# Mixer loads on GpSimd's queue with two buffers, alternating pooling inputs and gates, held-back last-block products, and a shorter VectorE chain for the samples

## The chip, the cores and the metric

One core of one Trainium2 chip runs the whole kernel. The metric is the device time of one execution in microseconds; the median of three timed runs stands for the kernel. A profile is one further execution, taken by the hardware profiler. The engines are TensorE (PE in the profile, PEld its weight loads), VectorE (DVE), ScalarE (ACT), GpSimd (POOL) and SyncE (SP, which here only issues DMAs).

## What is computed

One layer of a streaming encoder, on 1024 prompt positions and on 8 samples of 16 new positions with 1024 cached ones. All is float32.

```python
xn = rms_norm(x, norm_g)
u, g_pool, c_q, c_kv, k_r, g_mla = jnp.split(xn @ w_in, SPLIT_IDX, axis=-1)
pool_out = multiscale_pool(pool_hist, u, pos0, w_pool, pool_scale) * jax.nn.silu(g_pool)
q = (rms_norm(c_q, q_norm_g) @ w_uq).reshape(B, T, N_HEADS, D_NOPE + D_ROPE)
...
k_nope = rms_norm(kv[..., :D_NOPE], k_nope_g)
attn = chunk_causal_attention(q_nope, q_rope, k_nope, krope_all, v, q_pos, jnp.arange(S))
mla_out = attn.reshape(B, T, D_MLA) * jax.nn.silu(g_mla)
h = x + jnp.concatenate([pool_out, mla_out], axis=-1) @ w_out
gate = jax.nn.sigmoid(rms_norm(h, ple_norm_g) @ w_ple_gate + b_ple_gate)
y = h + gate * (p @ w_ple)
```

`multiscale_pool` takes 1024 channels in four groups of 256. For group g it forms the mean of the last 2, 4, 8 or 16 rows of u, subtracts u, multiplies by the group's 256 x 256 matrix and scales the channels.

## The kernel before

Positions lie along the free dimension: 1152 columns in NT = 3 blocks of TB = 384, of which the first two are prompt and the third ends with the 128 sample columns. A float32 product is made of three products of rounded halves (`split` makes the halves: ScalarE the high one, VectorE the low one; `mm3` and `product` multiply).

**Phase 1** (`phase1`) makes the input projection in tiles of 128 output channels. `kinds` lists 30 such tiles in order: 2 of ckv, 4 of cq, 8 gates gp, 8 pooling inputs u, 8 gates gm. The 2048 input rows are taken in two chunks c = 0 and 1. For the first two position blocks two tiles at a time are made with seven products in place of eight (`Quick.pair`, of 12 matmuls each, whose combined weights `sums` prepares one pair ahead). The third block, X, is multiplied plainly: 24 matmuls a tile (`product` with n = 8). In chunk 0 `keep` stores partial results; in chunk 1 `prior` loads them into PSUM and `finish` adds, applies the row factor or the SiLU, and stores the tile in DRAM. A pair with X thus has 7 x 12 + 2 x 24 = 132 matmuls, a pair without 84.

In chunk 1 the pairs 0 to 5 are made, then waiting generators are run empty and a pool of tiles is closed, then the pairs 6 to 13 and last the pair 14, whose X products come after the operands' memory is released (`left.close()`), between the second phase's first loads and its first matmuls.

**The pooling mixer** (`Pool`) runs between the products. `mixer` is called between products of the pairs 6 to 14 and does two steps per call. At pairs 8 to 11 it appends the 13 steps of one group: for each of the three blocks two `tile` (load u, sliding sums in `window`, difference d), one `mix` of the block before (L718 to L727: load the gate, six matmuls of the group's matrix, product of PSUM, scale and gate at L726, store), one `split` of d. u, the gate tile "ev", d and its halves have one buffer each; `aux_bank` has two PSUM banks. All loads and stores here are issued by SyncE, whose queue issues in order.

**Phase 2** makes keys, values and queries (`phase2`); its weights and latents come through raw tiles with two buffers. Phase 3 is the prompt's attention, phase 4 the samples' (`attend_samples`), phase 5 the output projection and the gate.

**The samples' attention** goes over 8 samples b and two halves f of four key tiles j (64 in all). Per key tile TensorE writes a three-bank PSUM tile: eight heads' keys (1024 columns), 128 score columns and 256 rotary ones. ScalarE squares the keys into sq (L1316, L1317), VectorE sums them by head (L1318), ScalarE copies the scores (L1319). Per half VectorE makes reciprocal roots (`rsqrt`, L86 to L90) and multiplies the scores of each key tile (L1324); GpSimd adds the rotary parts. `queries` splits the rotary queries of one sample into "qhl". `weigh` then does the softmax and the values of the sample before.

The order of instructions on each engine is laid down when the kernel is built, from a simulated timeline and the order in the program; on the chip each engine then runs its list in order.

Of the kernel before, what the change touches and what calls it, by code (L numbers as in the profile page):

```python
# [14 lines left out]
D = 2048  # L15
# [23 lines left out]
class K:  # L39
# [53 lines left out]
    def spread(self, pool, ps, out, r):  # L93

        nc = self.nc
        n = r.shape[1]
        rb = self.t(pool, [P, n, P], "sq")
        nc.vector.tensor_copy(rb[:], r[:].unsqueeze(2).to_broadcast([P, n, P]))
        for j in range(n):
            nc.tensor.transpose(ps[:, j * P:(j + 1) * P], rb[:, j, :], self.ident[:])  # L100
        nc.scalar.activation(out[:], ps[:, :n * P], AF.Copy)
# [151 lines left out]
def phase1(k, sc):  # L253
# [22 lines left out]
    kinds += [(n, i) for n in ("gp", "u", "gm") for i in range(8)]  # L276
# [45 lines left out]
    def factors(pool, acc, n, dim, wait=1):  # L322

        a = aux_bank()
        for j in range(n):
            nc.tensor.matmul(a[:, j:j + 1], acc[:, j * P:(j + 1) * P], k.ones[:, :1], start=True, stop=True)
        v = k.t(pool, [P, n], f"fv{n}")
        r = k.t(pool, [P, n], f"fr{n}")
        nc.vector.tensor_scalar(v[:], a[:, :n], 1.0 / dim, EPS, ALU.mult, ALU.add)
        k.rsqrt(pool, r[:], v[:], f"frs{n}")  # L330
        for _ in range(wait):
            yield
        for j in range(0, n, 3):
            k.spread(pool, aux_bank(), acc[:, j * P:(j + 3) * P], r[:, j:j + 3])
# [136 lines left out]
    def chunk(c, prior, done, between, pairs=pairs):  # L471
        def weights(m):
            return qk.sums(src[2 * m:2 * m + 2], c, c or 2 * m >= EARLY)

        W = weights(pairs[0])
        for m in pairs:
# [3 lines left out]
            qk.pair(2 * m, 2 * m + 1, A, X if c or 2 * m >= EARLY else None, W, prior, done, lambda i: between(m, i))  # L480
            W = Wn

    def prepare(m, i):
# [5 lines left out]
        if i == 1 and m == 4:  # L489
            k.later(factors(ep, R2, 3, D))  # L490
# [27 lines left out]
    def finish(i, t, ps, q):  # L518
# [18 lines left out]
        else:  # L537
            sq = k.t(lp, [P, 3, P], "sq")
            nc.scalar.activation(sq[:].rearrange("p a b -> p (a b)"), o[:], AF.Square)
            nc.vector.tensor_tensor(acc[kind, t][0][:], acc[kind, t][0][:], sq[:].rearrange("p a b -> p (a b)"), ALU.add)  # L540
# [3 lines left out]

    def ticks(m, i):
        k.tick()
# [5 lines left out]
    chunk(1, prior, finish, ticks, range(6))  # L552
    while k.queue:
        k.tick()
    ls.close()


    mp = es.enter_context(tc.tile_pool(name="p1p", bufs=1, side="right", reuse_waits="tile"))
    inv = k.t(mp, [P, 16], "inv")
    nc.sync.dma_start(inv[:], io["inv_cnt"])  # L560
    pool = Pool(k, mp, aux_bank, inv, sc, wp)

    def mixer(m, i):
        if 8 <= m < 12 and i == 0:
            g = m - 8
            for t in range(NT):
                steps.extend([lambda c=c, t=t: pool.tile(2 * g + c, t) for c in range(2)])
# [4 lines left out]
                steps.append(pool.split)  # L572
# [3 lines left out]
    chunk(1, prior, finish, mixer, range(6, KR // 2 - 1))  # L576
# [3 lines left out]
    qk.tail()  # L580
    left.close()
    yield
    for i in range(2):
        e = bank()[:, :TB]
        nc.scalar.activation(e, prior(2 * last + i, 2)[:], AF.Copy)
        qk.product(e, X, W["rest"][i], False, 8)
        finish(2 * last + i, 2, e, None)
# [61 lines left out]
class Pool:  # L649


    def __init__(self, k, pp, aux_bank, inv, sc, wp):
        self.k, self.pp, self.aux, self.inv, self.sc = k, pp, aux_bank, inv, sc
        self.wp, self.hl, self.d = wp, [None, None], [None, None]

# [25 lines left out]

    def tile(self, ct, t):
        k, pp, nc, io = self.k, self.pp, self.k.nc, self.k.io
        src = self.sc["u"]
# [4 lines left out]
        u = k.t(pp, [P, HIST + TB], "u")  # L689
        if t == 0:  # L690
            nc.gpsimd.memset(u[:, :HIST], 0.0)  # L691
        else:
            nc.sync.dma_start(u[:, :HIST], src[t - 1][:, ct, TB - HIST:])
        nc.sync.dma_start(u[:, HIST:], src[t][:, ct, :])
# [562 lines left out]
def attend_samples(k, sc, sh, between, fill):  # L1257
# [13 lines left out]
    KW = 448  # L1271
    wkh, wkl, qp, qr, lnew, cnw = sh.wkh, sh.wkl, sh.qp, sh.qr, sh.lnew, sh.cnw
# [26 lines left out]
    def scores(b, f, l, q, ch, cl, ks):  # L1299
# [3 lines left out]
        for j in range(HK):  # L1303
# [10 lines left out]
            sh.last = nc.tensor.matmul(ps[:, 2, 2 * P:], ks[:, c], qhl[:], start=True, stop=True)  # L1314
# [339 lines left out]
```

## Time and profile before

| | us |
|---|---|
| median of three runs | 2329.97 |
| lowest and highest run | 2327.18, 2331.05 |
| the profiled execution, whole | 2347.59 |
| its span, first to last instruction | 2345.8 |

| engine | busy in the span |
|---|---|
| TensorE | 95% |
| TensorE's weight loads | 92% |
| VectorE | 63% |
| ScalarE | 42% |
| GpSimd | 13% |

The mean granted TensorE clock is 0.976. Busy time of an engine in a stretch is read from tables by stretch; a pause of an engine is put down to the instruction that released it last. Matmuls overlap, so the spacing of their starts tells more than their durations.

### The profile page before, as it was taken

The numbers are of one execution on the slowest core, as the hardware profiler recorded it, in microseconds if no ns is written. First come the engines' busy times: TensorE is split into PE (matmuls) and PEld (weight loads), VectorE is DVE, ScalarE is ACT, GpSimd is POOL, SyncE is SP. The second block draws the span as 40 slices with busy tenths as digits, with TensorE's granted clock in tenths as the row PEclk, the third lists the DMA queues.
The fourth block names the chain that finished last, engine by engine and source line by source line (L and its number), as shares of the span: only waits on it lengthen the run. The fifth ranks groups of instructions, "written<-read, shape, count | busy, mean of one in ns | idle before, by whom it ended". The sixth has DMA issues, their size and how long they took to land.

```text
span 2345.8 us, 35907 instructions
## 1 busy us (share of the span) xinstructions
PE 2232.0 (95%) x12856; PEld 2168.6 (92%) x12856; DVE 1472.4 (63%) x3096; ACT 975.2 (42%) x2117; POOL 316.4 (13%) x261
## 2 busy tenths in 40 slices
PE   8989999999888979989999799999999999999999
PEld 7989999999888869878988689999999999999998
DVE  6787776775566667867898865555553336344343
ACT  6533335443223256666655454343342234223222
POOL 0000000000000000005444442222002221111110
PEclk9999999999998999999999889999999999999999
DMA  8574447454566585464221564444353334223222
GB/s 291 179 246 150 126 126 222 154 167 153 153 169 164 149 267 161 140 206 121 76 90 50 181 205 147 129 150 130 104 183 113 105 102 131 88 84 100 88 82 65
DMA packets 262355, 337.15 MB, mean 144 GB/s; under 512 B 46752, under 2 KB 215072, under 8 KB 262176
## 3 DMA queue, kind: packets, MB, share of 16 engines
q1 hardware_dynamic: 242880, 311.64, 43.8%
q10 hardware_dynamic: 19296, 23.21, 3.0%
q8 instruction: 101, 1.65, 0.3%
q14 instruction: 78, 0.64, 0.1%
HBM read 233.64 MB, written 101.12 MB: 143 GB/s over the span
## 4 chain that ended last, share of the span: by engine, by line
PE 50%; DVE 8%; DMA 8%; issue 2%; ACT 1%; POOL 0%; SPq 0%; ACTq 0%; DVEq 0%; POOLq 0%
PE mm L77 8%; PE mm L79 8%; PE mm L78 8%; PE f L77 3%; PE f L79 3%; PE f L78 3%; PE k L79 2%; PE k L78 2%; PE k L77 2%; PE t L1190 1%; DMA ev<-gp 1%; PE pb L77 1%; PE s L78 1%; PE s L77 1%; PE pb L79 1%
## 5 line engine op out<-in xcount | busy, mean ns | idle before, releaser
L68 ACT ACTIVATE wh<-wraw 128x1024 fp32r<-128x1024 f32 (+3 forms) x233 | 178.7, 769 | 233.3 <-PE mm L177 141.9
L69 DVE TENSOR_TENSOR wl<-wraw,wh 128x1024 fp32r<-128x1024 f32 (+3 forms) x231 | 205.8, 892 | 64.8 <-ACT wh L68 61.8
L1510 DVE TENSOR_TENSOR ev<-mm,R 128x384 f32<-128x384 f32 x48 | 26.7, 556 | 173.7 <-PE mm L79 169.8
L1511 ACT ACTIVATE ev<-ev,gains 128x384 f32<-128x384 f32 x48 | 29.4, 612 | 224.5 <-DVE ev L1510 124.4
L71 ACT ACTIVATE wh<-wraw,gains 128x128 fp32r<-128x128 f32 x256 | 82.1, 391 | 52.8 <-ACT wh L71 31.6
L691 POOL MEMSET u<- 128x15 f32 x8 | 0.9, 111 | 764.1 <-DVE kr L610 490.6
L72 DVE SCALAR_TENSOR_TENSOR wl<-wraw,gains,wh 128x128 fp32r<-128x128 f32 x256 | 87.2, 386 | 19.2 <-ACT wh L71 18.3
L77 PE MATMUL k<-wkh,ch 128*128 128x448 f32 x256 | 96.3, 377 | 2.5 <-ACT ch L68 1.4
L1191 ACT ACTIVATE pth<-t 128x512 fp32r<-128x512 f32 (+2 forms) x96 | 45.5, 485 | 127.9 <-PE t L1190 126.7
L78 PE MATMUL k<-wkh,cl 128*128 128x448 f32 x256 | 95.5, 373 | 0.5 <-DVE cl L69 0.5
L79 PE MATMUL k<-wkl,ch 128*128 128x448 f32 x256 | 94.8, 370 | 0.0
L1318 DVE TENSOR_REDUCE v<-sq 128x8 f32<-128x1024 f32 x64 | 77.7, 1213 | 14.5 <-ACT sq L1317 14.2
L79 PE MATMUL mm<-A2l,wh 128*128 128x384 f32 x256 | 86.1, 336 | 0.0
L78 PE MATMUL mm<-A2h,wl 128*128 128x384 f32 x256 | 86.1, 336 | 0.0
L77 PE MATMUL mm<-A2h,wh 128*128 128x384 f32 x256 | 86.0, 336 | 0.0
L1316 ACT ACTIVATE sq<-k 128x896 f32<-128x896 f32 x64 | 58.5, 914 | 66.0 <-PE k L1314 61.9
L77 PE MATMUL mm<-A0h,wh 128*128 128x384 f32 x256 | 85.8, 335 | 0.0
L79 PE MATMUL mm<-A0l,wh 128*128 128x384 f32 x256 | 85.7, 335 | 0.0
L78 PE MATMUL mm<-A1h,wl 128*128 128x384 f32 x256 | 85.7, 335 | 0.0
L78 PE MATMUL mm<-A0h,wl 128*128 128x384 f32 x256 | 85.7, 335 | 0.0
L79 PE MATMUL mm<-A1l,wh 128*128 128x384 f32 x256 | 85.5, 334 | 0.0
L77 PE MATMUL mm<-A1h,wh 128*128 128x384 f32 x256 | 85.5, 334 | 0.0
(796 smaller groups left out, 7787.6 us busy)
## 6 DMA issues: line engine op xcount, KB each, us to landing
wraw<-w_in SPq DMA_DIRECT2D x85, 512.0 KB, 4.6
part<-o SPq DMA_DIRECT2D x93, 192.0 KB, 2.7
q<-part SPq DMA_DIRECT2D x93, 192.0 KB, 3.0
wraw<-w_out SPq DMA_DIRECT2D x64, 256.0 KB, 3.4
wraw<-w_ple_gate SPq DMA_DIRECT2D x64, 256.0 KB, 3.1
ple<-ev ACTq DMA_DIRECT2D x48, 192.0 KB, 3.3
fev<-xT SPq DMA_DIRECT2D x48, 192.0 KB, 2.5
hp<-fev SPq DMA_DIRECT2D x48, 192.0 KB, 1.9
```

What stands on the lines that cost most here:

```text
L68: nc.scalar.activation(hi, src, AF.Copy)
L69: eng.tensor_tensor(lo, src, hi, ALU.subtract)
L71: nc.scalar.activation(hi, src, AF.Copy, scale=scale)
L72: eng.scalar_tensor_tensor(lo, src, scale, hi, ALU.mult, ALU.subtract)
L77: mm(out, sh, mh, start=start, stop=False)
L78: mm(out, sl, mh, start=False, stop=False)
L79: self.last = mm(out, sh, ml, start=False, stop=stop)
L1191: nc.scalar.activation(pth[:, :n, qq], tp[:, :n, :], AF.Copy)
L1316: nc.scalar.activation(sq[:, :2 * KW].rearrange("p (g c) -> p g c", g=2), ps[:, :2, :KW], AF.Square)
L1318: nc.vector.tensor_reduce(v[:, j, :], sq[:].rearrange("p (h d) -> p h d", h=H), AX.X, ALU.add)
L1510: nc.vector.tensor_tensor(g[:], ps[:, :TB], R[t][:], ALU.mult)
L1511: nc.scalar.activation(g[:], g[:], AF.Sigmoid, bias=k.b_ple_gate[:, ct:ct + 1])
```

## The change

`kinds` is ordered by groups: gp 0, gp 1, u 0, u 1, gp 2, gp 3, u 2, u 3 and so on, then gm. Chunk 1 is one run over the pairs 0 to 13; the mixer's groups are appended at pairs 5, 7, 9 and 11. The u loads (`fetch`) and the gate loads (`gates`) are issued by GpSimd, each with two buffers, as steps of their own ahead of use. The pairs 12 and 13 leave out their X products, as pair 14 did; all six tiles are multiplied after the release, four of them with weights loaded and split again. In the samples' attention the rotary queries of two samples are split at once; VectorE sums seven heads by a reduce and ScalarE the eighth by its accumulator; the four multiplications of a half become one. The buffer of `spread` gets a name as argument, and some tiles are declared flat.

```diff
-        rb = self.t(pool, [P, n, P], "sq")
-        nc.vector.tensor_copy(rb[:], r[:].unsqueeze(2).to_broadcast([P, n, P]))
+        rb = self.t(pool, [P, n * P], tag)[:].rearrange("p (n q) -> p n q", n=n)
+        nc.vector.tensor_copy(rb, r[:].unsqueeze(2).to_broadcast([P, n, P]))
...
-    kinds += [(n, i) for n in ("gp", "u", "gm") for i in range(8)]
+    kinds += [(n, 2 * g + i) for g in range(4) for n in ("gp", "u") for i in range(2)]
+    kinds += [("gm", i) for i in range(8)]
...
-            k.later(factors(ep, R2, 3, D))
+            k.later(factors(ep, R2, 3, D, tag="u3"))
...
-    def chunk(c, prior, done, between, pairs=pairs):
+    def chunk(c, prior, done, between, pairs=pairs, plain=KR):
+        def whole(m):
+            return 2 * m < plain if c else 2 * m >= EARLY
+
         def weights(m):
-            return qk.sums(src[2 * m:2 * m + 2], c, c or 2 * m >= EARLY)
+            return qk.sums(src[2 * m:2 * m + 2], c, whole(m))
...
-            qk.pair(2 * m, 2 * m + 1, A, X if c or 2 * m >= EARLY else None, W, prior, done, lambda i: between(m, i))
+            qk.pair(2 * m, 2 * m + 1, A, X if whole(m) else None, W, prior, done, lambda i: between(m, i))
...
-    chunk(1, prior, finish, ticks, range(6))
-    while k.queue:
+    def mixer(m, i):
         k.tick()
-    ls.close()
...
+        if m < 5:
+            return
+        if not mix:
+            assert not k.queue
+            ls.close()
...
-        if 8 <= m < 12 and i == 0:
-            g = m - 8
+        if m in (5, 7, 9, 11) and i == 0:
+            g = (m - 5) // 2
             for t in range(NT):
-                steps.extend([lambda c=c, t=t: pool.tile(2 * g + c, t) for c in range(2)])
+                if t == 0:
+                    pool.fetch(2 * g, 0)
+                steps.append(lambda t=t: (pool.fetch(2 * g + 1, t), pool.tile(2 * g, t)))
+                steps.append(lambda t=t: pool.tile(2 * g + 1, t))
                 if t:
                     steps.append(lambda t=t: pool.mix(g, t - 1))
                 else:
                     steps.append(lambda: pool.weights(g))
-                steps.append(pool.split)
+                steps.append(lambda t=t: (pool.gates(g, t), t < NT - 1 and pool.fetch(2 * g, t + 1), pool.split()))
             steps.append(lambda: pool.mix(g, NT - 1))
         step(2)
 
-    chunk(1, prior, finish, mixer, range(6, KR // 2 - 1))
+    chunk(1, prior, finish, mixer, range(KR // 2 - 1), KR - 2 * 3)
...
     qk.tail()
+    wn = (qk.hl(qk.raw(src[KR - 2 * 3], 1)), 0)
     left.close()
     yield
-    for i in range(2):
+
+    held = [2 * last, 2 * last + 1] + list(range(KR - 2 * 3, 2 * last))
+    for n, i in enumerate(held):
+        w = W["rest"][n] if n < 2 else wn
+        if 1 < n < len(held) - 1:
+            wn = (qk.hl(qk.raw(src[held[n + 1]], 1)), 0)
         e = bank()[:, :TB]
-        nc.scalar.activation(e, prior(2 * last + i, 2)[:], AF.Copy)
-        qk.product(e, X, W["rest"][i], False, 8)
-        finish(2 * last + i, 2, e, None)
+        nc.scalar.activation(e, prior(i, 2)[:], AF.Copy)
+        qk.product(e, X, w, False, 8)
+        finish(i, 2, e, None)
         step(len(steps))
...
+    def fetch(self, ct, t):
+
+        k, nc, src = self.k, self.k.nc, self.sc["u"]
+        u = self.u[ct, t] = k.t(self.pp, [P, HIST + TB], "u", bufs=2)
+        if t == 0:
+            nc.vector.memset(u[:, :HIST], 0.0)
+        else:
+            nc.gpsimd.dma_start(u[:, :HIST], src[t - 1][:, ct, TB - HIST:])
+        nc.gpsimd.dma_start(u[:, HIST:], src[t][:, ct, :])
+
+    def gates(self, g, t):
+        k = self.k
+        for n in (2 * g, 2 * g + 1):
+            self.gate[n, t] = k.t(self.pp, [P, TB], "ev", bufs=2)
+            k.nc.gpsimd.dma_start(self.gate[n, t][:], self.sc["gp"][t][:, n, :])
...
-            gate = k.t(pp, [P, TB], "ev")
-            nc.sync.dma_start(gate[:], sc["gp"][t][:, n, :])
+            gate = self.gate.pop((n, t))
...
         m = m3[b % 2]
+        if b % 2 == 0:
+            qhl[0] = k.t(kb, [P, 2, 2 * NQ], "qhl", F32R, bufs=2)
+            k.split(qhl[0][:, :, :NQ], qhl[0][:, :, NQ:], qr[:, b:b + 2, :])
         k.split(m[0][:, :, P:], m[1][:, :, P:], qp[:, :, b, :])
-        qhl = k.t(kb, [P, 2 * NQ], "qhl", F32R, bufs=2)
-        k.split(qhl[:, :NQ], qhl[:, NQ:], qr[:, b, :])
-        return m, qhl
+        return m, qhl[0][:, b % 2, :]
...
-            sq = k.t(kb, [P, H * DN], "sq", bufs=2)
-            nc.scalar.activation(sq[:, :2 * KW].rearrange("p (g c) -> p g c", g=2), ps[:, :2, :KW], AF.Square)
-            nc.scalar.activation(sq[:, 2 * KW:], ps[:, 2, :P], AF.Square)
-            nc.vector.tensor_reduce(v[:, j, :], sq[:].rearrange("p (h d) -> p h d", h=H), AX.X, ALU.add)
+            sq = k.t(kb, [P, 2 * KW], "sq", bufs=2)
+            junk = k.t(kb, [P, DN], "junk")
+            nc.scalar.activation(sq[:].rearrange("p (g c) -> p g c", g=2), ps[:, :2, :KW], AF.Square)
+            nc.scalar.activation(junk[:], ps[:, 2, :P], AF.Square, accum_out=v[:, j, H - 1:])
+            nc.vector.tensor_reduce(v[:, j, :H - 1], sq[:].rearrange("p (h d) -> p h d", h=H - 1), AX.X, ALU.add)
...
-        for j in range(HK):
-            nc.vector.tensor_tensor(heads(l[:, f * HK + j, :]), heads(ls[:, j, :NQ]),
-                                    r[:, j, :].unsqueeze(2).to_broadcast([P, H, NS]), ALU.mult)
         lv = l[:, f * HK:(f + 1) * HK, :]
+        nc.vector.tensor_tensor(lv.rearrange("p k (h s) -> p k h s", s=NS),
+                                ls[:, :, :NQ].rearrange("p k (h s) -> p k h s", s=NS),
+                                r[:].unsqueeze(3).to_broadcast([P, HK, H, NS]), ALU.mult)
```

## Rows read from the trace of the kernel before

**Rows 1.** The page's first part: busy us, share of the span, instructions.

```profile
PE 2232.0 (95%) x12856; PEld 2168.6 (92%) x12856; DVE 1472.4 (63%) x3096; ACT 975.2 (42%) x2117; POOL 316.4 (13%) x261
```

**Rows 2.** By stretch: length, busy us (instructions) PE, PEld, DVE, ACT, POOL, clock, DMA.

```profile
548.00:594.00 46.00, 46.00 (x264) 46.00 (x263) 24.65 (x37) 16.82 (x27) 0.11 (x1) 1.00 0.49 153
594.00:630.00 36.00, 36.00 (x207) 36.00 (x206) 21.65 (x39) 9.35 (x14) 0.00 (x0) 1.00 0.51 145
630.00:818.00 188.00, 155.39 (x812) 152.26 (x811) 126.73 (x251) 51.49 (x89) 0.67 (x6) 0.90 0.64 161
818.00:835.00 17.00, 12.15 (x60) 11.83 (x59) 5.65 (x11) 3.83 (x10) 0.00 (x0) 0.80 0.63 192
835.00:880.00 45.00, 35.98 (x157) 28.85 (x158) 33.48 (x86) 29.20 (x88) 0.00 (x0) 0.92 0.91 286
1045.00:1300.00 255.00, 244.81 (x1456) 230.53 (x1455) 217.14 (x420) 157.24 (x308) 117.27 (x69) 0.98 0.29 93
```

**Rows 3.** TensorE's timeline: start us, us, line, operation, tiles, idle before.

```profile
645.19 0.66 PE L77 MATMUL aux<-dh,pwh 128*128 128x384 f32 x1 [10.96 <-DVE ev L726]
...
645.97 0.52 PE L176 MATMUL mm<-X2h,wl 128*128 128x384 f32 x1
646.29 0.52 PE L177 MATMUL mm<-X2l,wh 128*128 128x384 f32 x1
```

**Rows 4.** Waits from 630 to 818: who, for whom, us, times, longest.

```profile
DVE s L675 <- DMA u<-u: 25.8, 12, 6.3
...
PE aux L77 <- DVE ev L726: 25.5, 6, 11.0
...
DVE ev L726 <- DMA ev<-gp: 21.0, 12, 5.3
```

**Rows 5.** Waits of SyncE's own queue from 630 to 818.

```profile
SPq L721 <- DMA mixp<-ev: 29.0, 16, 6.3
```

**Rows 6.** DMA issues from 594 to 830: count, KB each, median us to landing.

```profile
wraw<-w_in SPq DMA_DIRECT2D x10, 512.0 KB, 5.2
mixp<-ev SPq DMA_DIRECT2D x24, 192.0 KB, 2.4
u<-u SPq DMA_DIRECT2D x23, 192.0 KB, 3.0
ev<-gp SPq DMA_DIRECT2D x23, 192.0 KB, 2.4
```

**Rows 7.** TensorE's timeline where the second phase begins.

```profile
834.87 0.79 PE L77 MATMUL pb<-wkh,ckvh 128*128 128x512 f32 x1 [4.85 <-ACT ckvh L68]
```

**Rows 8.** The DMAs that touch the tiles u, 594 to 830.

```profile
DMA to landing us min/median/max: 1.4/2.7/8.1
```

**Rows 9.** VectorE's groups from 594 to 830: count, busy us, mean ns, idle before.

```profile
L69 DVE TENSOR_TENSOR wl<-wraw,wh 128x1024 fp32r<-128x1024 f32 x19 | 23.1, 1218 | 1.6 <-ACT wh L68 1.6
...
L679 DVE SCALAR_TENSOR_TENSOR d<-s,u 128x384 f32<-128x384 f32 x15 | 8.3, 552 | 0.1
...
L158 DVE TENSOR_TENSOR wt<-wraw,wraw 128x512 f32<-128x512 f32 x6 | 4.2, 692 | 7.7 <-DMA wraw<-w_in 7.7
...
L706 DVE COPY us<-u 128x128 f32<-128x128 f32 x8 | 1.8, 220 | 0.0
```

**Rows 10.** Groups of the samples' attention, 1045 to 1300.

```profile
L1318 DVE TENSOR_REDUCE v<-sq 128x8 f32<-128x1024 f32 x64 | 77.7, 1213 | 14.5 <-ACT sq L1317 14.2
...
L1324 DVE TENSOR_TENSOR l<-ls,r 128x128 f32<-128x128 f32 x60 | 19.7, 389 | 0.2
...
L69 DVE TENSOR_TENSOR qhl<-qr,qhl 128x128 fp32r<-128x128 f32 x6 | 11.6, 1933 | 0.2
```

**Rows 11.** ScalarE's accumulator reads in the second phase, 818 to 1030.

```profile
L854 ACT ACTIVATION_READ_ACCUMULATOR sq<-qn 128x1 f32 x72 | 13.9, 192 | 0.0
```

**Rows 12.** Waits in the samples' attention, 1045 to 1300.

```profile
ACT sq L1316 <- PE k L1314: 61.9, 37, 5.1
...
PE aux L1366 <- DVE r L86: 5.8, 3, 2.5
```

More of the change, by code (lines that the diff above doesn't have):

```diff
@@ L90, in rsqrt, with spread @@
             ve.scalar_tensor_tensor(y, a[:], 1.5, y, ALU.add, ALU.mult)
-    def spread(self, pool, ps, out, r):
+    def spread(self, pool, ps, out, r, tag="sq"):
         nc = self.nc
         n = r.shape[1]
-        rb = self.t(pool, [P, n, P], "sq")
-        nc.vector.tensor_copy(rb[:], r[:].unsqueeze(2).to_broadcast([P, n, P]))
+        rb = self.t(pool, [P, n * P], tag)[:].rearrange("p (n q) -> p n q", n=n)
+        nc.vector.tensor_copy(rb, r[:].unsqueeze(2).to_broadcast([P, n, P]))
         for j in range(n):
@@ L320, in squares, with factors @@
             nc.vector.tensor_tensor(acc[:], acc[:], sq, ALU.add)
-    def factors(pool, acc, n, dim, wait=1):
+    def factors(pool, acc, n, dim, wait=1, tag="sq"):
         a = aux_bank()
@@ L333, in factors @@
         for j in range(0, n, 3):
-            k.spread(pool, aux_bank(), acc[:, j * P:(j + 3) * P], r[:, j:j + 3])
+            k.spread(pool, aux_bank(), acc[:, j * P:(j + 3) * P], r[:, j:j + 3], tag)
     steps = []
@@ L537, in finish @@
         else:
-            sq = k.t(lp, [P, 3, P], "sq")
-            nc.scalar.activation(sq[:].rearrange("p a b -> p (a b)"), o[:], AF.Square)
-            nc.vector.tensor_tensor(acc[kind, t][0][:], acc[kind, t][0][:], sq[:].rearrange("p a b -> p (a b)"), ALU.add)
+            sq = k.t(lp, [P, TB], "sq")
+            nc.scalar.activation(sq[:], o[:], AF.Square)
+            nc.vector.tensor_tensor(acc[kind, t][0][:], acc[kind, t][0][:], sq[:], ALU.add)
         acc[kind, t][1] -= 1
@@ L543, in finish @@
             k.later(latent_factor(kind, t, acc[kind, t][0]))
-    def ticks(m, i):
-        k.tick()
     lp = ls.enter_context(tc.tile_pool(name="p1c", bufs=1, side="right", reuse_waits="tile"))
@@ L551, in phase1 @@
     rope_tables(k, lp, kc, ks, io["k_rope_g2"], 1.0)
-    chunk(1, prior, finish, ticks, range(6))
-    while k.queue:
+    mix = []
+    def mixer(m, i):
         k.tick()
-    ls.close()
[L558 to L563, printed above, removed]
-        if 8 <= m < 12 and i == 0:
-            g = m - 8
+        if m < 5:
[3 more added lines that the diff above has]
+            ls.close()
+            mp = es.enter_context(tc.tile_pool(name="p1p", bufs=1, side="right", reuse_waits="tile"))
+            inv = k.t(mp, [P, 16], "inv")
+            nc.sync.dma_start(inv[:], io["inv_cnt"])
+            mix.append(Pool(k, mp, aux_bank, inv, sc, wp))
+        pool = mix[0]
+        if m in (5, 7, 9, 11) and i == 0:
+            g = (m - 5) // 2
             for t in range(NT):
-                steps.extend([lambda c=c, t=t: pool.tile(2 * g + c, t) for c in range(2)])
+                if t == 0:
+                    pool.fetch(2 * g, 0)
+                steps.append(lambda t=t: (pool.fetch(2 * g + 1, t), pool.tile(2 * g, t)))
+                steps.append(lambda t=t: pool.tile(2 * g + 1, t))
                 if t:
@@ L654, in __init__ @@
         self.wp, self.hl, self.d = wp, [None, None], [None, None]
+        self.u, self.gate = {}, {}
     def weights(self, g):
@@ L680, in window @@
         return cur
+    def fetch(self, ct, t):
[11 more added lines that the diff above has]
+            k.nc.gpsimd.dma_start(self.gate[n, t][:], self.sc["gp"][t][:, n, :])
     def tile(self, ct, t):
         k, pp, nc, io = self.k, self.pp, self.k.nc, self.k.io
-        src = self.sc["u"]
         g, c2 = divmod(ct, 2)
@@ L688, in tile @@
         n = TB if t < NT - 1 else SEQ - TB * (NT - 1)
[L689 to L694, printed above, removed]
+        u = self.u.pop((ct, t))
         s = self.window(u[:, :HIST + n], n, d[:, :n], w)
@@ L1271, in attend_samples @@
     KW = 448
+    qhl = [None]
     wkh, wkl, qp, qr, lnew, cnw = sh.wkh, sh.wkl, sh.qp, sh.qr, sh.lnew, sh.cnw
@@ L1313, in scores @@
                     k.mm3(ps[:, g, :n], ch[:, rt, c], cl[:, rt, c], mh, ml, rt == 0, rt == 1)
-            sh.last = nc.tensor.matmul(ps[:, 2, 2 * P:], ks[:, c], qhl[:], start=True, stop=True)
-            sq = k.t(kb, [P, H * DN], "sq", bufs=2)
-            nc.scalar.activation(sq[:, :2 * KW].rearrange("p (g c) -> p g c", g=2), ps[:, :2, :KW], AF.Square)
-            nc.scalar.activation(sq[:, 2 * KW:], ps[:, 2, :P], AF.Square)
-            nc.vector.tensor_reduce(v[:, j, :], sq[:].rearrange("p (h d) -> p h d", h=H), AX.X, ALU.add)
+            sh.last = nc.tensor.matmul(ps[:, 2, 2 * P:], ks[:, c], qhl, start=True, stop=True)
+            sq = k.t(kb, [P, 2 * KW], "sq", bufs=2)
[3 more added lines that the diff above has]
+            nc.vector.tensor_reduce(v[:, j, :H - 1], sq[:].rearrange("p (h d) -> p h d", h=H - 1), AX.X, ALU.add)
             nc.scalar.activation(ls[:, j, :], ps[:, 2, P:], AF.Copy)
```

## The prediction

> **What bounds the kernel now.** I read the page first: TensorE is busy for 95% of the span [rows 1], so time can only come out of places where it idles or runs at the lower clock. Cutting the span into stages shows where [rows 2]. From 594 to 630 us it does 207 products in 36.0 us, 0.174 us each, without a gap: this is its pace. From 630 to 818 us the same products run, 812 of them, and should take 812 x 0.174 = 141 us; the stage lasts 188. So 47 us are lost there: 32.6 as idle time (188 - 155.4), the rest at the lower clock. The clock's share is visible in single products: after an idle 10.96 us the spacing is 0.32 us (645.97 to 646.29) instead of 0.174 [rows 3]; the granted clock of the stage is 0.90, a mixture of the level 2.4 GHz and of 1.2 GHz behind each such gap.
>
> That stage is where the pooling mixer runs between the input projections. The waits name its cause [rows 4]: TensorE stood 25.5 us in six waits for the product with the gate (L726), because a matmul into an auxiliary bank needs the bank's last occupant evicted, and the eviction is that product. VectorE itself stood 21.0 us for the gate's load and 25.8 us for the load of u. The queue's own waits show why the loads are late: SyncE's issue of the gate load stood 29.0 us until the previous mixed tile had been stored [rows 5]; both use the one buffer "ev", so store and next load follow each other (2.4 and 2.4 us to landing [rows 6]). u has one buffer too. While SyncE waits there, every other load and store behind it waits as well.
>
> Two more stages lose time [rows 2]: 818 to 880 us, where the second phase starts (17 - 60 x 0.174 = 6.6 us, then 9.0 us idle), with the largest gap of 4.85 us for the first latent block [rows 7]; and the samples' attention, 1045 to 1300 us, with 10.2 us idle.
>
> **The change, part by part.** The sums are made against the profiled execution (span 2345.8 us, 2347.6 us in all). It lies 17.6 us above the median of the runs shown, 2329.97; I take the saving over to the median unchanged.
>
> *The mixer.* The arithmetic stays: the same windows, splits, products. 24 gate loads and 24 + 16 loads of u leave SyncE's queue for GpSimd's, which in this stage is otherwise free (0.67 us busy [rows 2]). Both tiles get two buffers and are asked for one or more steps earlier. Alternating gates and inputs lets the four groups start after pairs 5, 7, 9 and 11 instead of 8 to 11: 13 steps for two pairs (16 slots) instead of 13 a pair, so they no longer pile up to the end. The drain and the first unprefetched weights between pairs 5 and 6 go too, but 548 to 594 us shows no idle TensorE worth counting, and I give them nothing.
> The new waits: on GpSimd's queue two gate loads wait for the stores of the tiles before them, and behind them stands the next u load, and behind that VectorE's next window, and behind that the weight splits and evictions that TensorE needs. Eight small memsets move from GpSimd to VectorE, hidden by the third of its time that is free. One step pair is about half a projection pair, 66 x 0.174 = 11.5 us. Store 2.4, load 2.4 and the next load 3.0 us, by SyncE's rows [rows 6], make 7.8 us, inside 11.5 but not by much. No row shows a load issued by GpSimd. Its cost is bounded below by SyncE's 2.4 to 3.0 us, above by the longest time to landing at that tile, 8.1 us [rows 8]; I take about 4, nearer to the ordinary row, because nothing else stands on that queue.
> Remaining loss: VectorE is busy 126.7 of 188 us [rows 2], two thirds, and the last group (four adding steps a window) meets pairs 12 and 13, which without their last-block products are 14.6 us long rather than 23. A few us of TensorE waiting there are likely. I leave 10 of the 47: gain 37, ends 15 and 45.
>
> The Trainium skill speaks against this queue: the page "SBUF — State Buffer", section "SBUF: two separate sides", in its box on the "DVE blocks DMA" trap, says that a DMA from GpSimd has its descriptors written by that engine, which is locked out while VectorE runs a copy in a two-port mode. The row that bears on it: in the stage only the 0.22 us copies x8 [rows 9] can be such an operation, so by the rule at most 1.8 us of delay, and the sum would be 35 instead of 37. The two engines do collide in this trace, though with VectorE as the loser: the rotary split of 128 columns averages 1.93 us beside GpSimd's arithmetic [rows 10].
>
> *Held-back products.* Six last-block products instead of two follow the release of the operands: 6 x 24 x 0.174 = 25.1 us of TensorE work instead of 8.4, while the second phase loads and splits its weights. TensorE's total is unchanged. The first gap (4.85 us) and the waits for value and query weights up to 880 us should be covered, since that phase is asked for 16.7 us earlier relative to TensorE. What is late next is the rest of its loads, which pass through two buffers one behind the other. Of 15.6 us I take 10; ends 17 (with the slow clock) and -3.
> Cost: four more weight loads of 512 KB, landing in 5.2 us [rows 6], and net three more splits (four whole ones less two halves), 1.22 us each on VectorE [rows 9]. The cover is the product before each: 4.2 us. If a load is asked for only one product ahead, 5.2 + 2.4 for the split (ScalarE's half taken like VectorE's 1.22) - 4.2 = 3.4 us stay open, four times, 13 us. I take nothing, because the first is asked for before the operands go and the others need no data, only buffers that are free by then; 13 - 10 gives the lower end.
>
> *Samples.* The reduce takes 1.213 us for 1024 columns [rows 10]; 128 fewer save the difference between a 512- and a 384-column operation, 0.692 - 0.552 = 0.14 us [rows 9], 64 times: 9 us. 64 multiplications of mean 0.389 us [rows 10], 25 us, become 16 of about 0.69: 11 us. Eight rotary splits of 1.93 us become four: some 7 us. VectorE sheds about 30 of its 217 us. ScalarE gains 64 accumulator reads of 0.19 us [rows 11], 12 us on 157 of 255, which lies beside TensorE. But TensorE is busy 244.8 us of the 255, and ScalarE waited 61.9 us for it [rows 12]: only the 10.2 us idle and some clock can come back, 5.8 of it waits behind VectorE's roots [rows 12]. I take 6; ends 13 and 0 (-12 if every accumulator read lay on the path, which 61.9 us of ScalarE waiting excludes).
>
> *The rest* (the spread's buffer under another name, flat tiles) frees memory and moves no work: 0, hidden by pairs that have no gap.
>
> Sum: 37 + 10 + 6 = 53 us. 2347.6 - 53 = 2294.6 in a profiled execution; 2330 - 53 = **2277** for the median. Own range 2255 (45 + 17 + 13) to 2297 (24 + 6 + 3).
>
> **The rivals.**
> *A, the wait moves into GpSimd's queue.* The u load behind two gate loads behind two stores comes just too late; VectorE stands at the window's first add as now, though TensorE no longer stands for the gate itself. For it: 7.8 us against 11.5 is a thin margin when a landing takes 8.1. Against it: the order on the queue may let u pass first, as u needs no store. Price: half of the mixer's gain stays, 18 + 8 + 4 = 30: 2300 us.
> *B, slower.* GpSimd's loads are slow in themselves, and each of the 24 windows waits. In the present kernel 46.8 us of VectorE waiting for u and gates (25.8 + 21.0 [rows 4]) went with 47 us lost on TensorE, one for one. The new loss equals today's 47 and the other 16 us together when 24 x s = 63, that is from a stall s of 2.6 us for each window; at 4 us it is 96 - 63 = 33 us slower: 2363. Against it: s is what remains after a lead of several us.
> *C, the change doesn't reach the end.* TensorE's order is fixed when the kernel is made; if idle time only moves to other stages, the time stays: 2330.
>
> **How the numbers follow.** Forecast 0.60, A 0.24, C 0.05, B 0.11. Two executions differ by up to 0.2%, about what can be told from no change. Faster by more: 0.84; within: 0.05; slower: 0.11. The range takes the forecast's lower end and A with some room above its 2300: 2256 to 2312; beyond lie B, C and little else.
>
> **What would show it.** TensorE's wait for the gate product, 25.5 us, under 5; the mixer's stretch with a granted clock of 0.97 or more and under 12 us idle; VectorE's waits for u under 15 us in all (over 50: B; between, with waits of gate loads for stores on GpSimd's queue: A). The second phase's first product without its 4.85 us gap; four more loads of input weights, none of the held products waiting over 1 us. The reduce at 1.07 us, and samples ending some 6 us sooner after their start. I am wrong if TensorE idles as long as now at the mixer, or if new gaps open in pairs 12 to 14.

## The result, and the profile after

The changed kernel takes 2300.94 us (median of 4 runs, 2295.69 to 2309.69) against 2330.51 for the kernel before beside it: ratio 0.9877, 95% interval 0.9841 to 0.9912, so 29.6 us less (20 to 37 by the interval) where 53 were forecast. In a second measurement it gave 2297.34 and 0.9861 (0.9841 to 0.988). Its profiled execution lasts 2295.69 us, with a span of 2293.9.

The page's first part, answering [rows 1]: TensorE's share has gone from 95 to 97%.

```profile
PE 2217.6 (97%) x12856; PEld 2160.4 (94%) x12856; DVE 1450.2 (63%) x3056; ACT 985.4 (43%) x2181; POOL 345.7 (15%) x317
```

By stretch, answering [rows 2]: the mixer from its first to its last pooling product (537 to 759), the held products (759 to 809), the start of the second phase, the samples.

```profile
537.00:759.00 222.00, 206.94 (x1124) 204.86 (x1123) 159.59 (x316) 73.14 (x122) 31.00 (x58) 0.95 0.68 182
759.00:809.00 50.00, 44.84 (x258) 44.55 (x257) 31.64 (x54) 22.43 (x38) 0.00 (x0) 0.98 0.77 238
809.00:880.00 71.00, 70.78 (x391) 66.04 (x391) 53.78 (x166) 50.99 (x181) 0.00 (x0) 0.96 0.63 191
1001.00:1246.00 245.00, 242.71 (x1466) 229.54 (x1467) 202.65 (x378) 162.78 (x370) 113.56 (x69) 1.00 0.33 103
```

Counted as in the prediction, the mixer loses 222 - 1124 x 0.174 = 26.4 us. The same stretch of the kernel before, in the execution from which I predicted:

```profile
606.00:822.00 216.00, 183.39 (x962) 180.26 (x961) 140.70 (x279) 56.79 (x97) 0.67 (x6) 0.91 0.62 158
```

And in a second execution of that same kernel:

```profile
606.00:808.00 202.00, 174.35 (x938) 170.83 (x937) 137.72 (x273) 56.70 (x97) 0.66 (x6) 0.94 0.62 166
```

216 - 962 x 0.174 = 48.6 us in the first, 202 - 938 x 0.174 = 38.8 in the second. The same kernel loses 10 us more in one profile than in the next; this second execution is the run b_again below.

The waits of the changed kernel's mixer, 537 to 759, beside [rows 4]: who, for whom, us in all, times, longest.

```profile
POOL u L704 <- DMA u<-o: 69.4, 8, 18.3
...
POOL ev L710 <- DMA mixp<-ev: 23.3, 8, 11.7
...
DVE s L689 <- DMA u<-u: 20.4, 9, 4.5
...
DVE wt L158 <- DMA wraw<-w_in: 14.0, 6, 4.4
...
DVE s L689 <- DMA us<-state_pool: 9.0, 3, 4.1
PE aux L77 <- DVE ev L749: 9.0, 2, 4.6
```

TensorE's wait for the gate product fell from 25.5 to 9.0 us, and VectorE's for the gate's load from 21.0 to nothing. But VectorE still stands 20.4 us for u, and 14.0 for the weights of the projection, which in the kernel before were 4.6. Over the mixer its waits for transfers come to 20.4 + 14.0 + 9.0 + 4.0 (npool<-us) + 3.1 (partial sums) + 1.0 (npool<-u) = 51.5 us; in the kernel before, from 606 to 822, they were 32.7 + 21.0 + 5.7 + 4.6 + 1.1 = 65.1, and 55.5 in its second execution. Most of the standing is still there.

What went is the standing at one place, the product with the gate, which also empties TensorE's bank. The second execution of the kernel before, 606 to 808:

```profile
DVE ev L726 <- DMA ev<-gp: 24.7, 14, 4.8
...
PE aux L77 <- DVE ev L726: 22.9, 5, 9.8
```

In the changed kernel no wait of VectorE for a gate is left.

Where VectorE stands for u shows what is left. VectorE's timeline, the window's first adds in the mixer's second group (start us, us, line, operation, tiles, idle before):

```profile
572.96 0.57 DVE L689 TENSOR_TENSOR s<-u 128x398 f32<-128x398 f32 x1 [4.53 <-DMA u<-u]
...
597.76 0.57 DVE L689 TENSOR_TENSOR s<-u 128x398 f32<-128x398 f32 x1 [2.46 <-DMA u<-u]
...
600.20 0.56 DVE L689 TENSOR_TENSOR s<-u 128x398 f32<-128x398 f32 x1
...
604.42 0.57 DVE L689 TENSOR_TENSOR s<-u 128x398 f32<-128x398 f32 x1
...
610.43 0.43 DVE L689 TENSOR_TENSOR s<-u 128x270 f32<-128x270 f32 x1
...
613.75 0.43 DVE L689 TENSOR_TENSOR s<-u 128x270 f32<-128x270 f32 x1
```

The first two of six stand, the other four don't: these two are the first block of the group's two tiles. In the third and fourth group it is the same (3.02 and 2.77 us; 3.83 and 1.58, with 0.8 once later). In the kernel before 16 of the 23 recorded ones stood, spread over the blocks. GpSimd's queue says for what the first ones come late:

```profile
551.53 0.54 POOL L710 DMA_DIRECT2D ev<-gp  x1 [3.11 <-DMA mixp<-ev]
570.27 0.54 POOL L704 DMA_DIRECT2D u<-u  x1 [18.21 <-DMA u<-o]
...
593.05 0.54 POOL L704 DMA_DIRECT2D u<-u  x1 [2.86 <-DMA u<-o]
```

The load at 570.27 stands 18.21 us for "u<-o", the store of the projection's product, which SyncE issued at 563.91; VectorE starts on its data at 572.96. The load at 593.05 waits for the last of the pair's six stores, issued at 588.15; VectorE starts on it at 597.76. A group's inputs are made by the pair of products just ahead of the group, and the first block of its second tile is the last that this pair stores.

### The profile page after: what moved, and what is told of

The parts are those of the page before. It is cut to its first block, busy times and chain, and to the rows that moved or that the text cites. A ratio compares the mean times of both kernels' runs of the same rounds, so it can differ in the third digit from the quotient of the medians.

```text
span 2293.9 us, 35989 instructions
## 1 busy us (share of the span) xinstructions
PE 2217.6 (97%) x12856; PEld 2160.4 (94%) x12856; DVE 1450.2 (63%) x3056; ACT 985.4 (43%) x2181; POOL 345.7 (15%) x317
## 4 chain that ended last, share of the span: by engine, by line
PE 54%; DMA 7%; DVE 6%; issue 2%; ACT 2%; POOL 1%; SPq 0%; ACTq 0%; DVEq 0%; POOLq 0%
PE mm L77 8%; PE mm L79 8%; PE mm L78 8%; PE f L77 3%; PE f L79 3%; PE f L78 3%; PE k L78 2%; PE k L79 2%; PE k L77 2%; PE t L1213 1%; DMA rawcq<-cq 1%; PE o L79 1%; PE o L78 1%; PE s L78 1%; PE s L79 1%
## 5 line engine op out<-in xcount | busy, mean ns | idle before, releaser
L69 DVE TENSOR_TENSOR wl<-wraw,wh 128x1024 fp32r<-128x1024 f32 (+3 forms) x235 | 210.6, 897 | 69.9 <-ACT wh L68 67.3
L704 POOL DMA_DIRECT2D u<-u x24 | 13.1, 544 | 602.1 <-DVE frs3a L88 509.3
L1498 DVE TENSOR_TENSOR ev<-mm,ev 128x384 f32<-128x384 f32 x48 | 26.8, 558 | 86.3 <-PE mm L79 85.9
```

What stands on the lines that cost most here:

```text
L69: eng.tensor_tensor(lo, src, hi, ALU.subtract)
L1498: nc.vector.tensor_tensor(h[:], ps[:, :TB], h[:], ALU.add)
```

## The experiments

Times of different chips are compared by their ratio to the kernel before (2330 to 2336 us on these chips), kernels measured side by side directly. Mixer loss is length less products x 0.174 us, from the first to the last pooling product; the expectations count idle time plus half of the busy time at the lower clock, which for most comes out 1 to 3.5 us less (24.9 for the changed kernel). "Stands" is the sum of VectorE's waits for transfers in that stretch.

| kernel | us | ratio (95%) | mixer loss | VectorE stands |
|---|---|---|---|---|
| before, second execution (b_again) | 2332.35 | | 38.8 | 55.5 |
| s_only | 2321.28 | 0.9964 (0.995-0.9978) | 41.9 | 57.4 |
| m_only | 2320.33 | 0.9957 (0.9943-0.997) | 25.0 | 52.7 |
| a_nohold | 2314.59 | 0.9931 (0.9915-0.9946) | 22.9 | 50.0 |
| a_sync | 2312.68 | 0.9903 (0.9886-0.992) | 43.1 | 61.8 |
| a_onebuf | 2318.70 | 0.993 (0.9913-0.9947) | 53.8 | 78.7 |
| a_us | 2307.40 | 0.9876 (0.9858-0.9895) | 31.4 | 56.5 |
| a_rot | 2299.12 | 0.9843 (0.9825-0.9861) | 29.8 | 54.6 |
| a_again | 2297.34 | 0.9861 (0.9841-0.988) | 24.7 | 54.1 |
| a_ufirst | 2286.43 | 0.981 (0.9792-0.9827) | 17.2 | 38.8 |
| a_best | 2283.63 | 0.9803 (0.9785-0.9822) | 15.3 | 30.9 |
| a_noalt | 2307.29 | 0.9898 (0.9879-0.9916) | 28.6 | 43.8 |

**The parts alone.** Four kernels: before once more (b_again), before with only the samples' part (s_only), before with only the mixer's part and the last pair held as before (m_only), and the changed kernel without the four additional held products (a_nohold):

```
-    chunk(1, prior, finish, mixer, range(KR // 2 - 1), KR - 2 * 3)
+    chunk(1, prior, finish, mixer, range(KR // 2 - 1), KR - 2)
...
-    held = [2 * last, 2 * last + 1] + list(range(KR - 2 * 3, 2 * last))
+    held = [2 * last, 2 * last + 1]
```

> The kernel before, profiled once more beside the others. The profiled execution that the prediction used took 2347.6 us, 17 us over its timed runs. If that surplus was a disturbance of that one execution, this one has a span near 2328 us and loses less than 47 us between 630 and 818 us; if the mixer always loses 47 us there, the span is near 2346 us again.

> The kernel before with the samples' part of the change alone. By the prediction 6 us less than before (between 0 and 13): ratio 0.997. Rival: ScalarE's 64 accumulator reads of 0.19 us lie on the path, up to 12 us more: ratio up to 1.005. In the trace the reduce is at 1.07 us and the four multiplications of a half are one of about 0.7 us.

> The kernel before with the mixer's part alone: order of the tiles, GpSimd's queue, two buffers, one run over the pairs, but only pair 14's products held back, and the samples as before. By the prediction 37 us less (15 to 45): ratio 0.984. If the loss of the kernel before was smaller in its timed runs than in its first profile, 20 to 25 us less: ratio 0.990.

> The changed kernel without the held-back products of the pairs 12 and 13 (pair 14's stay held back, as before). By the prediction 10 us slower than the changed kernel, ratio to before about 0.992. Rival, from the trace of the changed kernel, in which a gap of 5.16 us still stands before the second phase's first product although its weights were split 14 us earlier: the products cover nothing that ends last, since that first product waits for the PSUM banks, which VectorE frees late; then this kernel takes the time of the changed one within 4 us, ratio about 0.988.

The samples' part is worth 8.4 us (0.36% of 2330), the mixer's 10.0 (0.43%), holding back four more products 0.9931 - 0.9877 = 0.54%, 13 us (16 against a_again's 0.9861). The three make 31 to 35 and the whole 29.6: they add up within the intervals. So one term of the sum is far off in size, the mixer's: 10 us in time (7 to 13) instead of 37, and less than the 20 to 25 expected from a smaller starting loss. Its loss did fall, from 38.8 or 48.6 to 25.0; the other executions of the unchanged mixer (38.8, 41.9) say that the larger of the two starting points belongs to that one profile.

What fell there isn't VectorE's standing as a whole: 55.5 us in b_again and 57.4 in s_only, 52.7 in m_only. TensorE's wait for the gate product fell, from 22.9 us in b_again to 4.7 in m_only, 538 to 756:

```profile
PE aux L77 <- DVE ev L746: 4.7, 1, 4.7
```

That isn't the whole either: a_sync, below, loses 43.1 us with 2.9 us of such waits for a gate.

The held products show in the profiles too. From the mixer's end to the samples a_nohold loses 265 - 1317 x 0.174 = 35.8 us, the changed kernel 242 - 1281 x 0.174 = 19.1 (its row stands under **Without the alternation**):

```profile
753.00:1018.00 265.00, 243.83 (x1317) 224.08 (x1316) 183.80 (x530) 154.23 (x493) 1.95 (x8) 0.95 0.56 170
```

**Queue or buffers.** a_sync gives the loads back to SyncE and keeps the second buffers; a_onebuf keeps GpSimd and takes the second buffers and the early requests away.

```
a_sync:    -        nc.gpsimd.dma_start(u[:, HIST:], src[t][:, ct, :])
           +        nc.sync.dma_start(u[:, HIST:], src[t][:, ct, :])
           ...
           -            k.nc.gpsimd.dma_start(self.gate[n, t][:], ...)
           +            k.nc.sync.dma_start(self.gate[n, t][:], ...)
a_onebuf:  -        u = self.u[ct, t] = k.t(self.pp, [P, HIST + TB], "u", bufs=2)
           +        u = self.u[ct, t] = k.t(self.pp, [P, HIST + TB], "u")
           ...
           -            self.gate[n, t] = k.t(self.pp, [P, TB], "ev", bufs=2)
           +            self.gate[n, t] = k.t(self.pp, [P, TB], "ev")
```

> The changed kernel with the mixer's input and gate loads issued by SyncE again; second buffers, order of issue and all other parts stay. Theory (the second buffers carry the mixer's gain, the queue little): the mixer stage, from the first pooling operation to the last, loses 24 to 29 us of TensorE (24.9 in the changed kernel), and the time is 2298 to 2306 us. Rival (the queue carries it, since weights and history loads stand behind the gate loads' waits on SyncE): the loss is 31 us or more, the time 2307 to 2313.

> The changed kernel with one buffer each for the pooling input and the gate, allocated and loaded at the places where the kernel before does it, but issued by GpSimd; all other parts stay. Theory (the second buffers carry it): the mixer stage loses 32 to 38 us, as in the kernel before (35.8 and 46.9 in its two profiles), and the time is 2308 to 2316 us. Rival (the queue carries it): 24 to 28 us of loss and 2298 to 2305 us.

a_sync is 12 to 15 us slower than the changed kernel in time, by the ratio 6 to 10 (its interval overlaps that of the changed kernel's first measurement, not that of a_again); it went as the rival said. a_onebuf came out worse than both theories had it, 53.8 us lost. In both the mixer loses at least as much as in b_again, so neither half carries the gain alone. SyncE's own queue in a_sync shows what stands there, 538 to 777:

```profile
SPq L710 <- DMA mixp<-ev: 24.5, 13, 5.1
SPq L512 <- DMA q<-part: 20.1, 8, 5.3
SPq L704 <- DMA u<-o: 17.5, 9, 3.6
```

The gate loads wait for the mixed tiles' stores and the inputs for their products' stores, now on the queue that also carries the weights. VectorE's waits in the same stretch:

```profile
DVE wt L158 <- DMA wraw<-w_in: 23.9, 6, 6.8
DVE u L234 <- DMA q<-part: 13.7, 4, 5.1
DVE s L689 <- DMA u<-u: 12.1, 7, 2.8
```

It stands less for u (12.1 against 20.4), and more for weights and partial sums (37.6 against 17.1): by these rows the queue move helps what stands behind these loads, more than the loads themselves. In a_onebuf the two old waits are back, on the other queue, 537 to 801:

```profile
DVE s L687 <- DMA u<-u: 29.6, 16, 4.7
DVE ev L748 <- DMA ev<-gp: 27.0, 8, 7.0
```

**The sample history.** The tile "us" still has one buffer, and its load waits for the store of the tile before; VectorE stood 13.0 us for the two. a_us gives it two buffers and loads it with the third block's input:

```
     nc.gpsimd.dma_start(u[:, HIST:], src[t][:, ct, :])
+    if t == NT - 1:
+        us = self.us[ct] = k.t(self.pp, [P, NB, HIST + NS], "us", bufs=2)
+        nc.sync.dma_start(us[:, :, :HIST], k.io["state_pool"][ct])
...
-            us = k.t(pp, [P, NB, HIST + NS], "us")
-            nc.sync.dma_start(us[:, :, :HIST], io["state_pool"][ct])
+            us = self.us.pop(ct)
```

> The changed kernel with two buffers for the sample-history tile us, its state_pool load issued with the fetch of the third block's input instead of after the earlier tile's npool store. Theory (what is left of the mixer's loss comes from the single us tile: its load waits for the store of the tile before, VectorE stands, and the gate multiply and TensorE behind it): VectorE's waits for state_pool and npool go from 13 us to under 3, the mixer stage loses 13 to 18 us instead of 24.9, and the time is 2290 to 2295 us. Rival (the waits for the u loads, 19 us on VectorE now, take its place): the loss stays 21 us or more and the time 2297 to 2303.

The 13.0 us went, and the time didn't. VectorE's waits in a_us, 538 to 765:

```profile
DVE s L689 <- DMA u<-u: 20.9, 8, 5.1
DVE wt L158 <- DMA wraw<-w_in: 16.8, 7, 5.0
DVE u L234 <- DMA q<-part: 9.6, 4, 6.6
DVE us L732 <- DMA u<-u: 4.8, 3, 2.3
DVE u L701 <- DMA npool<-u: 4.4, 1, 4.4
```

56.5 us in all instead of 51.5: by these rows it gets to the next late transfer sooner and stands there. The mixer loses 31.4 us, and the ratio, 0.9876, is the changed kernel's. This theory fell; the rival held.

**The second phase's first product.** TensorE still stands 5.16 us ahead of it (4.85 in [rows 7]). VectorE's timeline in the changed kernel just before:

```profile
806.82 0.95 DVE L69 TENSOR_TENSOR wql<-raw,wqh 128x768 fp32r<-128x768 f32 x1
807.68 0.34 DVE L844 SCALAR_TENSOR_TENSOR rawcq<-rawcq,gains,srow 128x128 f32<-128x128 f32 x1
807.95 0.55 DVE L529 TENSOR_TENSOR o<-mm,R 128x384 f32<-128x384 f32 x1
```

TensorE's timeline at the same place:

```profile
803.15 0.34 PE L177 MATMUL mm<-X7l,wh 128*128 128x384 f32 x1
808.65 0.76 PE L77 MATMUL pb<-wkh,ckvh 128*128 128x512 f32 x1 [5.16 <-DVE o L529]
```

The last held product ends at 803.5. Its PSUM bank is the one that the second phase takes first, and its eviction (L529, 807.95) stands on VectorE behind that phase's own scalings and splits. a_rot moves that phase to another bank by taking two tiles of another tag first:

```
     pp = es.enter_context(tc.tile_pool(name="p2p", bufs=1, space=PSUM, ...))
+    for _ in range(2):
+        bank("pt")
```

> The changed kernel with two PSUM tiles of the transposes' tag taken and left unused ahead of the second phase's first product, so that this product goes into a bank that the last held-back product doesn't hold. Theory (the 5.16 us gap of TensorE ahead of the second phase is the wait for that bank's eviction, which stands on VectorE behind the second phase's own splits): the first second-phase product follows the last held-back one within 0.7 us, the loss from there to the samples falls from 13.3 to 8 to 10, and the time is 2294 to 2298 us. Rival (the weights of the second phase are late anyway): the gap is only moved by some products, the time stays 2299 to 2303.

The gap is gone, so it was the wait for that bank. Another of 3.69 us stands 11 us later, for the split of the weights of another product, p @ w_ple; TensorE's timeline in a_rot:

```profile
805.25 0.34 PE L177 MATMUL mm<-X7l,wh 128*128 128x384 f32 x1
805.42 0.39 PE L77 MATMUL pb<-wkh,ckvh 128*128 128x512 f32 x1
...
816.12 0.69 PE L77 MATMUL p<-h,wh 128*128 128x384 f32 x1 [3.69 <-ACT wh L68]
```

From the mixer's end to the samples it loses 18.8 us, against 19.1 and 18.9 in the changed kernel and a_again: the gap has only moved, as the rival said. Its time, 2299.12, is that of the changed kernel; by the ratio it gained 0.2 to 0.3%, with intervals that overlap. Whether it is worth anything stays open.

**The inputs a pair earlier.** a_ufirst exchanges the order of a group's two pairs, and a_best adds a_us and a_rot to that; a_again is the yardstick.

```
-    kinds += [(n, 2 * g + i) for g in range(4) for n in ("gp", "u") for i in range(2)]
+    kinds += [(n, 2 * g + i) for g in range(4) for n in ("u", "gp") for i in range(2)]
```

> The changed kernel once more, unaltered, as the yardstick beside the two others of this job: 2296 to 2306 us, 0.986 to 0.9895 of the kernel before, a mixer loss of 20 to 30 us (24.9 in its first profile).

> The changed kernel with one word exchanged: in each group the pooling inputs' pair of products comes before the gates' pair, so the inputs are stored a pair (some 27 us) earlier and the gates just in time. Theory (a new wait took the old one's place: since inputs and gates alternate, each group's first input load waits on GpSimd for the store of the product that makes it, and VectorE stands for it): VectorE's waits for the input loads between the mixer's first 540 to 765 us go from 20 us to under 9, its waits for all transfers there from 51 to under 42, the mixer stage loses 15 to 20 us, and the time is 4 to 8 us under the changed kernel's in the same job. Rival (VectorE only moves on to its next late transfer: weights, partial sums, sample history, as in the run with two history tiles): the sum of its waits stays above 45 us and the time within 3 us of the changed kernel's.

> The changed kernel with the free PSUM bank for the second phase's first product, two sample-history tiles with their load ahead, and the inputs' products ahead of the gates'. Theory (the gains add): 9 to 15 us under the changed kernel of the same job, 2285 to 2292 us. Rival (VectorE's waits replace one another; only the free bank counts): 4 to 8 us under it, 2293 to 2297.

Two words exchanged take off 10.9 us (2297.34 to 2286.43), more than the theory asked for; 7.5 of them are in the mixer's loss. The mixer's row in a_ufirst, by stretch:

```profile
539.00:746.00 207.00, 196.82 (x1091) 194.60 (x1090) 153.73 (x302) 69.96 (x119) 27.72 (x52) 0.98 0.69 188
```

Who waits for what in the same stretch, VectorE alone:

```profile
DVE wt L158 <- DMA wraw<-w_in: 10.8, 6, 2.4
...
DVE s L689 <- DMA u<-u: 8.6, 5, 4.0
DVE s L689 <- DMA us<-state_pool: 7.3, 3, 3.1
DVE wt L158 <- DMA q<-part: 7.3, 2, 4.6
DVE u L234 <- DMA q<-part: 4.8, 2, 2.9
```

VectorE stands 38.8 us instead of 54.1 (a_again), and for u 8.6 instead of 24.5; the loss is 207 - 1091 x 0.174 = 17.2 instead of 24.7. The gates, now just in time, cost VectorE nothing: GpSimd's gate loads stand 30.7 us for their products' stores, and no wait of VectorE for a gate is among its rows. a_best is the fastest, 2283.63, 2% under the kernel before. It lies 13.7 us under a_again, inside the 9 to 15 of its theory, but 10.9 of them are a_ufirst's: over that kernel it gains 2.8 us, with intervals that overlap. That the gains of a_us and a_rot add is not shown.

**Without the alternation.** The last run puts the products back in the old order and the groups at pairs 8 to 11, and keeps the rest:

```
-    kinds += [(n, 2 * g + i) for g in range(4) for n in ("gp", "u") for i in range(2)]
-    kinds += [("gm", i) for i in range(8)]
+    kinds += [(n, i) for n in ("gp", "u", "gm") for i in range(8)]
...
-        if m in (5, 7, 9, 11) and i == 0:
-            g = (m - 5) // 2
+        if 8 <= m < 12 and i == 0:
+            g = m - 8
```

> The changed kernel without the alternation: the products in the order of the kernel before (all gates, all pooling inputs, then the last kind), the mixer's four groups in the four consecutive pairs 8 to 11; second buffers, GpSimd's queue, held-back products and the samples' part stay. The inputs are again made one pair ahead of their group. Theory (the alternation carries part of the gain, since it gives the mixer's work on VectorE every second pair to recover in): the mixer stage loses 28 to 36 us, 2305 to 2314 us. Rival (second buffers and queue carry it alone, and the spacing is worth nothing): the loss stays 20 to 26 us, 2296 to 2303.

2307.29, some 5 to 9 us behind the changed kernel by the ratio, with intervals that overlap; the time is where the theory had it, but the mixer's loss (28.6) is near the changed kernel's (26.4 and 24.7), as the rival said. From the mixer's last product to the samples, in a_noalt:

```profile
806.00:1009.00 203.00, 184.96 (x1032) 168.34 (x1030) 157.52 (x486) 133.57 (x457) 2.63 (x8) 0.98 0.60 181
```

And in the changed kernel:

```profile
759.00:1001.00 242.00, 228.17 (x1281) 213.29 (x1279) 180.49 (x520) 154.09 (x489) 1.96 (x8) 0.98 0.61 186
```

203 - 184.96 = 18.0 us idle against 242 - 228.17 = 13.8: with the alternation the mixer ends 50 us ahead of the second phase, whose loads can be under way meanwhile; that this is the cause is a reading that no run tests. These 4 us and the mixer's 2 to 4 make up the difference; no single wait carries it. The alternation has a price as well: in a_noalt, from 606 to 806, no load of u on GpSimd's queue stands for an input's store, in the changed kernel eight do.

## Why the prediction was right or wrong

**The bound** was read rightly: the mixer was where time could come from, and the wait for the gate product its mark. The range of 2256 to 2312 held the time, because it took in rival A; the sum's own range, up to 2297, did not. (Its 24 + 6 + 3 are not the lower ends given for the three terms, 15, -3 and 0, which make 2318.) The forecast was 24 us too low.

**The mixer, 37 of 47, is the term that failed,** at 10.0 us alone, below its lower end of 15. By the losses 47 - 38.8 = 8 us of the missing 27 were not there to gain, and 25.0 - 10 = 15 stayed; of the 14 by which the loss fell, 10 show in the time. Three things are in it:
- The 47 us were one execution's. By the same count that profile loses 48.6 and the next 38.8. I carried the saving of the profiled execution over to the median "unchanged", although it lay 17.6 us above it; some 10 of these were in this stage of that one execution, so the median didn't have them to give. Between profiled executions the change gave 2347.59 - 2295.69 = 51.9, close to the 53 forecast, which is luck: the mixer's loss fell by 22 there, not by 37. Between medians it gave 29.6.
- "I leave 10": 26.4 and 24.7 stayed. The prediction listed the new waits as stores of the gate's buffer and gate loads ahead of u. It left out that u's load reads what the pair before has just made; 18.2 of VectorE's 20.4 us for u are at the first blocks of the last three groups. Making the inputs one pair earlier took VectorE's wait for u from 24.5 to 8.6 us and 7.5 us off the mixer's loss, which shows that part of the cause.
- VectorE works its list in order, and its standing for one transfer hides that the next would be late as well. I counted its waits for u and gates, 46.8 us, as the whole; when they shrank, weights rose from 4.6 to 14.0 and the sample history from 5.7 to 13.0. a_us removes 13.0 and gains nothing. Nor does the sum of its waits tell TensorE's loss: 55.5 us went with 38.8 lost in b_again, 52.7 with 25.0 in m_only.

**GpSimd's load at about 4 us** was right: 4.0 to landing for u, 4.7 for gates (2.9 and 2.6 from SyncE in a_sync). The Trainium skill's rule on VectorE locking GpSimd out (page "SBUF — State Buffer", section "SBUF: two separate sides") was weighed at 1.8 us. Moving the loads to GpSimd's queue gained time against a_sync. Each of GpSimd's 43 issues of these loads took 536 to 538 ns, and the waits before them are put down to data or buffers; whether the delay that the rule names is in the 1.1 to 2.1 us by which they land later than SyncE's, no run here shows.

**Rival A** gave the right time, 2300, and by the test set down (VectorE's u waits between 15 and 50 us, gate loads waiting for stores on GpSimd's queue, 23.3 us) it is what happened. But the agreement in time is luck: its 30 us were 18 + 8 + 4, and the parts measured 10, 13 to 16 and 8.4. And its mechanism, u behind gate loads that wait for mixed tiles, isn't what the queue shows: the first loads of u stand for their own inputs' stores (69.4 us). "u needs no store" was said against it, and u does need one, its own.

**Held-back products:** 10 forecast, 13 to 16 measured, inside the ends, by one of the two waits named. The first gap was to be covered, and stands at 5.16 us, as PSUM is freed late; what was covered are the waits behind it: 45 - 35.98 = 9.0 us idle from 835 to 880 in the kernel before [rows 2], 0.2 us from 809 to 880 now. The four more weight loads cost nothing that shows: the held stretch idles 50 - 44.84 = 5.2 us, all of it that gap.

**Samples:** 6 forecast, 8.4 measured. The reduce takes 1.079 us (1.07 expected) and the 512-column multiplication 0.690 (0.69), as their rows show:

```profile
L1344 DVE TENSOR_REDUCE v<-sq 128x7 f32<-128x896 f32 x63 | 68.0, 1079 | 10.3 <-ACT sq L1342 10.1
...
L1350 DVE TENSOR_TENSOR l<-ls,r 128x512 f32<-128x512 f32 x15 | 10.4, 690 | 0.4
```

Of 10.2 us idle 2.3 are left, and the stage's clock is 1.00 instead of 0.98. The rotary splits were misread: 1.93 us is the mean of six of the eight. All eight took 12.2 us in the kernel before, the four that replace them 1.7 in the changed one, so 10.5 us went instead of some 7 (min/median/max in ns, the kernel before and the changed one):

```profile
L69 DVE TENSOR_TENSOR qhl<-qr,qhl x8: 278/2178/2382, 1039.1 to 1237.2; 128x128 fp32r<-128x128 f32 x8
...
L69 DVE TENSOR_TENSOR qhl<-qr,qhl x4: 414/416/418, 996.6 to 1131.7; 128x256 fp32r<-128x256 f32 x4
```

**Rivals B and C** fell: 9 windows stand, for 20.4 us together, and the end moved.

**The other marks:** TensorE's wait for the gate product 9.0 (under 5 forecast), granted clock of the mixer 0.95 (0.97; a_again has 0.97), idle 15.1 (under 12): each missed in the direction of a load that is still late. No new gap opened at the pairs 12 to 14: from 715 to 804 TensorE waits 0.2 us.

## What to carry to other kernels

A second buffer takes away the wait for the buffer, and nothing else: before counting a load as early, follow what it reads back to the instruction that makes it, and if that is a product of the same kernel, put the producer further ahead. Count all transfers for which an in-order engine stands, not the two largest, since one that is gone can uncover the next; and look where it stands: with nearly the same standing m_only lost 25.0 us and b_again 38.8, of whose standing 24.7 us was at the product that empties TensorE's bank. And take a stage's loss from more than one execution before it is spent against a median.

## What the runs showed of the hardware that was not expected

A load issued by GpSimd took 0.54 us of that engine for each issue and 4.0 us to landing at the median, against 2.9 for the same 192 KB from SyncE in a_sync, at a DMA share of 0.64 to 0.68 in both. The Trainium skill (page "DMA: Bandwidth & Descriptors", section "Anatomy of one DMA — SWDGE (gpsimd) path") fits 2.0 us plus the bytes over 436e3 a us, by which an estimate for 192 KB is 2.45 us; the measurement, on busy DMA engines, is 1.5 us above. VectorE's rotary split of 128 columns took 0.28 or 0.29 us three times and 2.18 to 2.38 us five times in the kernel before; each of the five ran beside a split of 1024 columns on GpSimd (from 1109.54 beside GpSimd's at 1108.91, for example), none of the three did, and none of the changed kernel's four. And the same mixer lost 38.8, 41.9 and 48.6 us in three profiled executions (b_again, s_only, before), a spread as large as the measured gain of the mixer's part.
